# Output projection of an RG-LRU layer: the middle four of six channel groups from scaled two-byte halves

## The chip, the cores and the metric

One core of one Trainium2 chip runs the whole program. The metric is the device time of one execution in microseconds (us), taken as a median over runs. TensorE is PE in the profile (its weight loads are PEld), VectorE is DVE, ScalarE is ACT, GpSimd is POOL, and SyncE, which issues most DMA transfers, is SP.

## The reference, cut to what matters

The program computes two residual layers on a sequence of 1024 vectors of 1024 channels, and a final RMS norm. The change touches the first layer alone:

```python
def lru_mixer(h, w_in, conv_w, conv_b, wa, ba, wx, bx, a_param, w_out):   # h = rms_norm(x, g)
    u = h @ w_in                                     # 1024 -> 2 * 1536
    xb, gate = u[..., :LRU_WIDTH], u[..., LRU_WIDTH:]
    xc = causal_depthwise_conv(xb, conv_w, conv_b)   # 4 taps
    r = sigmoid(block_diag_linear(xc, wa, ba))       # 12 blocks of 128
    i = sigmoid(block_diag_linear(xc, wx, bx))
    a = exp(-LRU_C * r * softplus(-a_param))
    bterm = sqrt(1 - a * a) * (i * xc)
    hs = scan(a, bterm)                              # h_t = a_t * h_(t-1) + b_t
    y = hs * silu(gate)
    return y @ w_out                                 # 1536 -> 1024
```

All of it is float32. The second layer is attention with a forget gate, and the change leaves it alone.

## The kernel before, in words

**Precision.** Each large product of the first layer is made of three TensorE products. A float32 operand is split into a high part rounded to the four-byte type fp32r and a low part, the rest; `gemm_steps` (L141) then sums high by high, low weight by high activation, and high weight by low activation. Weights are split by a cast on ACT (`to_hi`, tile `wh`) and a subtraction (`to_lo`, tile `wl`), which POOL does for the input projection and DVE for the output projection. The second layer uses two-byte halves (fp16) scaled by bounds instead.

**Tiling.** The layer's 1536 inner channels are 12 blocks of 128, and the loop over n at L482 goes through them. Channels lie on the partitions and the 1024 positions along the free axis, in two halves of 512. A round n does this:

- `ups` of block n (the convolution's input, L490 and L504): 8 tiles of k, 2 halves and 3 products, so 48 matmuls of 128x128 by 512. `conv(n)` (L318) scales it by the row's inverse norm into `us`, and applies the four taps into `xc`.
- `gates(n-1)` (L337): 12 matmuls, and a tanh of each result on ACT (`th`, `ti`).
- `outputs(n-2)` (L383): y = a * sg on DVE, its high half `yh` by ACT and its low half `yl` by DVE.
- `gps` of block n-1 (the gate branch), 48 matmuls, `silu`, and `recur(n-1)` (L360): tanh, exp, square and sqrt on ACT, several DVE products, and the scan over the sequence on DVE (L380).

The output projection goes by groups of two blocks (`project_out(g)`, L405). A group is 16 `ops` tiles (8 output blocks, 2 halves) of 6 matmuls, each added to the residual `x` by DVE (L413). They fill the gaps between the other products: the code takes a few at a time (`take(fill, 2)`) in a later round.

`squares_of_weights` (L424) reads the second layer's weights during the first layer and sums their squares with ACT (tile `wsf`), which the second layer's scales need. It takes turns with `conv` for two small buffers (tag `wgf`). A call of `some()` (L476) brings one such step.

**What sets the order.** The framework's scheduler puts the instructions of each engine in an order from the data dependencies, from the buffers of each pool and from hints that one instruction be issued after another (`tc.issue_after`). Each engine then runs its own queue in that order. `ups` and `gps` share two PSUM tiles of two banks each (tag `S`), so `ups` of block n+1 cannot begin before DVE has read `ups` of block n. The `ops` tiles have two banks (tag `g`) and the gates two (tag `O`). The temporaries `us` and `m` (tag `m2`, the `t` of `recur`) each have one buffer.

Of the kernel before, what the change touches and what calls it, by code (L numbers as in the profile page):

```python
# [19 lines left out]
P = 128  # L20
# [7 lines left out]
GROUP = 2  # L28
ORDER = "1.v1..1.v1..00", "1.v1..1.v1..0000"
# [14 lines left out]
def trunk(ctx: ExitStack, tc: tile.TileContext, xt, w0, wg, wo0, pc, gn, gf, w1, wv, wf, bf, wo1, out):  # L44
# [163 lines left out]
    with nullcontext(ExitStack()) as l0:  # L208
# [106 lines left out]
        def product(pt, h, w):  # L315
            gemm(pt, zip(w, raw[h]))

        def conv(n, ups):  # L318
            us, xc = long("us"), long("xc", bufs=2)
# [40 lines left out]
        def recur(n, parts=(slice(0, SEQ),)):  # L360
# [4 lines left out]
            for cs in parts:  # L365
# [11 lines left out]
                with tc.issue_after(s["last"].ins):  # L377
                    nc.scalar.activation(t_, t_, AF.Sqrt, scale=1.0 / 16.0)
                nc.vector.tensor_tensor(ti, ti, t_, ALU.mult)
                nc.vector.tensor_tensor_scan(a_, a_, ti, old, ALU.mult, ALU.add)  # L380
                old = a[:, cs.stop - 1 : cs.stop]

# [22 lines left out]
        def project_out(g):  # L405

            for d0 in range(0, KT, 2):
                for db, w in enumerate(out_weights(g, d0), d0):
                    for h, cs in enumerate(halves):
                        pt = ps.tile([P, HALF], F32, tag="g", name="ops")  # L410
                        gemm(pt, zip(w, [tuple(z[:, cs] for z in p) for p in ys[2 * g : 2 * g + 2]]))
                        x = xs[h][db]
                        nc.vector.tensor_tensor(x, x, pt, ALU.add)  # L413
                        yield
# [7 lines left out]
        wsq = const.tile([P, 96], F32, name="wsq")  # L422

        def squares_of_weights():  # L424
# [8 lines left out]
            todo.append((wf, [root[:, 1:2]]))  # L433
            held = []
            for src, to in todo + [(None, None)]:
                if len(held) == 2 or src is None and held:
                    measure(*held.pop(0))
                if src is None:
                    break
                n = src.shape[1] * src.shape[2]  # L440
                wt = tmp.tile([P, HALF], F32, tag="wgf", name="wsf", bufs=2)[:, :n]
                nc.sync.dma_start(wt.rearrange("p (a b) -> p a b", b=src.shape[2]), src)
                held.append((wt, n // len(to), to))
                yield
# [37 lines left out]
        for n in range(NB):  # L482
# [7 lines left out]
            product(ups[0], 0, wu)  # L490
# [7 lines left out]
            else:  # L498
                gates(n - 1)
                if n > 1:  # L500
# [3 lines left out]
            product(ups[1], 1, wu)  # L504
# [8 lines left out]
            if n % 2 and n > 1:  # L513
# [13 lines left out]
            if n:  # L527
                drain(silu(state[n - 1], held.pop(n - 1)))

                with tc.issue_after(state[n]["tap"].ins):  # L530
                    recur(n - 1)
# [965 lines left out]
```

## Time and profile before

| what | value |
|---|---|
| median of 3 runs (lowest, highest) | 1024.79 us (1023.81, 1027.17) |
| the profiled execution's own time | 1025.09 us |
| its span, first to last instruction | 1023.2 us |
| mean granted TensorE clock | 0.995 |
| busy in the span: PE, PEld, DVE | 98%, 64%, 78% |
| busy in the span: ACT, POOL | 66%, 11% |

The first layer takes about the first 457 us. In the page, a group of instructions is named by its line, engine, operation and tiles (out<-in). In the timeline the columns are the start in us, the duration in us, the engine, the line, the operation and the tiles; a bracket at a row's end gives the engine's idle time ahead of it and what ended that. Matmuls overlap: the distance between the starts of two neighbours, called the pitch here, is what one costs TensorE, and it is shorter than the duration shown.

### The profile page before, as it was taken

The page shows a single profiled execution, that of the slowest core. Times are in us where ns is not written, and L with a number is a line of the kernel's source. Part 1 is how long each engine was busy: PE and PEld are TensorE (multiplying, and loading weights), DVE is VectorE, ACT ScalarE, POOL GpSimd, SP SyncE. Part 2 cuts the span into 40 slices and gives each one's busy share as a digit, 9 for nine tenths or more (in the row PEclk, how much of TensorE's full clock was granted, in tenths as well). Part 3 has the DMA queues.
Part 4 walks back from the last instruction along what each step waited for, and adds up shares of the span by engine and source line. Part 5 has one row for each costly group of instructions (what it writes and reads, how often), then busy time and mean ns, then how long its engine had stood idle before and what let it go on. Part 6 is the DMA issues. An engine that isn't in the chain of part 4 may idle for free.

```text
span 1023.2 us, 15101 instructions
## 1 busy us (share of the span) xinstructions
PE 999.1 (98%) x5098; PEld 656.1 (64%) x5098; DVE 794.3 (78%) x1504; ACT 672.7 (66%) x1215; POOL 110.4 (11%) x104
## 2 busy tenths in 40 slices
PE   9999999999999999999989999999999999998997
PEld 7787788788888887866545555555555555443454
DVE  7689585677558557998787889987888878995765
ACT  8469756657566667565775667766676666863555
POOL 1310221222122121000200000000010000001200
PEclk9999999999999999999999999999999999998999
DMA  7111433333334233252366677877687777778944
GB/s 254 62 52 49 140 121 107 98 119 125 98 104 149 93 106 103 80 170 95 82 156 130 119 161 153 177 155 147 134 202 138 151 140 150 155 166 183 244 78 166
DMA packets 219630, 135.88 MB, mean 133 GB/s; under 512 B 162080, under 2 KB 186464, under 8 KB 219552
## 3 DMA queue, kind: packets, MB, share of 16 engines
q1 hardware_dynamic: 216912, 126.27, 50.8%
q0 software_dynamic: 2640, 8.65, 3.3%
q8 instruction: 40, 0.66, 0.3%
q14 instruction: 38, 0.31, 0.1%
HBM read 75.16 MB, written 9.37 MB: 83 GB/s over the span
## 4 chain that ended last, share of the span: by engine, by line
PE 70%; DVE 10%; issue 8%; DMA 5%; ACT 4%; POOL 1%; SPq 1%; DVEq 0%; ACTq 0%; POOLq 0%
PE gps L72 26%; PE ops L72 14%; PE ups L72 10%; PE vps L72 7%; PE S L72 5%; PE O L72 4%; PE gate L72 2%; PE turn L72 1%; POOL wl L114 1%; DMA pT<-pp 1%; DMA wf<-in_w 1%; DVE w L733 1%; DMA wsf<-in_wo 1%; DVE h L660 1%; DVE pp L1088 1%
## 5 line engine op out<-in xcount | busy, mean ns | idle before, releaser
L72 PE MATMUL gps<-h,w 128*128 128x512 f16 x1152 | 268.1, 379 | 1.4 <-DVE qkl L902 0.7
L72 PEld LDWEIGHTS <-w 128*128 128x128 f16 x1440 | 140.6, 98 | 157.3 <-issue 7.3
L60 ACT ACTIVATE p<-p,m 128x128 f32<-128x128 f32 (+7 forms) x128 | 98.8, 772 | 74.4 <-DVE m L1075 70.1
L1075 DVE CUSTOM_DVE_ANT_0 p<-S,mask,vsq 128x128 f32<-128x128 f32 (+7 forms) x128 | 103.8, 811 | 21.1 <-PE S L72 19.6
L114 POOL TENSOR_TENSOR wl<-wf,wh 128x512 fp32r<-128x512 f32 x46 | 82.4, 1800 | 314.9 <-ACT wh L60 226.1
L60 ACT ACTIVATE pp<-p,sums 128x128 f16<-128x128 f32 (+7 forms) x128 | 97.9, 768 | 22.4 <-ACT p L60 14.5
L1088 DVE SCALAR_TENSOR_TENSOR pp<-p,sums,pp 128x128 f16<-128x128 f32 (+7 forms) x128 | 103.6, 812 | 10.9 <-ACT pp L60 10.5
L60 ACT ACTIVATE wsf<-wsf 128x512 f32<-128x512 f32 (+1 forms) x81 | 50.5, 625 | 61.7 <-DMA wsf<-in_w 33.5
L72 PEld LDWEIGHTS <-h 128*128 128x128 f16 x768 | 74.9, 98 | 21.5 <-issue 1.4
L72 PE MATMUL S<-T,U 128*128 128x512 f16 (+4 forms) x384 | 83.6, 327 | 1.4 <-DVE m L1075 1.1
L72 PE MATMUL ops<-yh,wh 128*128 128x512 f32 x192 | 76.7, 399 | 2.0 <-ACT yh L60 1.1
L72 PE MATMUL ups<-hh,wl 128*128 128x512 f32 x192 | 75.9, 395 | 0.8 <-POOL wl L114 0.8
L72 PE MATMUL ups<-hh,wh 128*128 128x512 f32 x192 | 76.4, 399 | 0.1
L72 PE MATMUL ups<-hl,wh 128*128 128x512 f32 x192 | 76.3, 397 | 0.2 <-DVE hl L275 0.2
L72 PE MATMUL ops<-yh,wl 128*128 128x512 f32 x192 | 75.7, 394 | 0.6 <-DVE wl L114 0.6
L72 PE MATMUL gps<-hh,wh 128*128 128x512 f32 x192 | 75.8, 395 | 0.0
L72 PE MATMUL gps<-hh,wl 128*128 128x512 f32 x192 | 75.5, 393 | 0.1
L72 PE MATMUL gps<-hl,wh 128*128 128x512 f32 x192 | 75.4, 393 | 0.0
L72 PE MATMUL ops<-yl,wh 128*128 128x512 f32 x192 | 74.5, 394 | 0.0
L413 DVE TENSOR_TENSOR x<-x,ops 128x512 f32<-128x512 f32 x80 | 53.7, 680 | 23.7 <-PE ops L72 23.5
L72 PE MATMUL vps<-wv,h 128*128 128x256 f16 x576 | 70.4, 273 | 0.0
L72 PE MATMUL ops<-y,w 128*128 128x512 f16 x288 | 69.2, 388 | 0.9 <-DVE sg L1044 0.9
(249 smaller groups left out, 1777.1 us busy)
## 6 DMA issues: line engine op xcount, KB each, us to landing
wf<-in_w SPq DMA_DIRECT2D x106, 256.0 KB
wsf<-in_w SPq DMA_DIRECT2D x48, 256.0 KB
wf<-in_wo SPq DMA_DIRECT2D x64, 128.0 KB
x<-in_xt SPq DMA_DIRECT2D x16, 256.0 KB
wsf<-in_wv SPq DMA_DIRECT2D x16, 256.0 KB
wsf<-in_wo SPq DMA_DIRECT2D x16, 256.0 KB
x1d<-x SPq DMA_DIRECT2D x16, 256.0 KB
T<-qkh SPq DMA_DIRECT2D x64, 64.0 KB
```

The costliest lines, as they stand in the source:

```text
L60: act[0] = op(*args, **kw)
L72: pe[0] = nc.tensor.matmul(*args, **kw)
L114: return eng.tensor_tensor(lo, src, f32(hi), ALU.subtract)
L413: nc.vector.tensor_tensor(x, x, pt, ALU.add)
L660: nc.vector.scalar_tensor_tensor(lo, x, g_, hi, ALU.mult, ALU.subtract)
L733: nc.vector.scalar_tensor_tensor(lo, wt, scale, hi, ALU.mult, ALU.subtract)
L1075: nc.vector.tensor_tensor_reduce(p, S[:, :n], mask[:, SEQ - n :], unit_s[:, pair : pair + 1], -NEG, ALU.add, ALU.min, accum_out=m)
L1088: nc.vector.scalar_tensor_tensor(both[:, :, 1], p, r, both[:, :, 0], ALU.mult, ALU.subtract)
```

## The change

Groups 1 to 4 of the output projection (blocks 2 to 9, the tuple `SCALED`) use fp16 halves; groups 0 and 5 stay as they are.

- After a = a * sg, ACT takes the absolute value of the whole row with a running sum per channel (`gate_output`). That sum gives a unit `u` per channel and its inverse. `scaled_output` makes the fp16 high half on ACT with that inverse as scale, and the low half on DVE.
- The squares of the group's weights are summed by the machinery of `squares_of_weights`: 16 more loads and 16 more squares on ACT. `weight_sum` and `weight_root` make a bound from them per partition.
- `group_scales` multiplies unit and bound, sums over all partitions by a small matmul against a tile of ones (`total`, which takes one of the two `g` banks), and derives the weights' scale and the result's unit on DVE.
- `scaled_out_weights` loads the weights as before and makes the fp16 halves with a scale per partition: two ACT casts of 256 columns and two DVE instructions in place of one of each with 512. It is called one step ahead. The eviction multiplies by the unit of the group while it adds.
- `conv`'s temporary `us` goes to the single buffer `m2` that `recur` uses. `product` calls `some` once more in its middle, for n from 3 to 10. `project_out` is made earlier in its round.

The small new tensors lie in old ones that are free by then: the channel units in `sp_d`, their inverses in `sp_q`, the weight bounds in `sp_e`, and the shares and units of a group in two columns of `pct`.

```diff
         def conv(n, ups):
-            us, xc = long("us"), long("xc", bufs=2)
+            us, xc = long("m2"), long("xc", bufs=2)
...
                 with tc.issue_after(s["last"].ins):
                     nc.scalar.activation(t_, t_, AF.Sqrt, scale=1.0 / 16.0)
+                    if root is not None:
+                        weight_root(root)
...
+        def gate_output(n):
+            s = state[n]
+            a_, u = s["a"], unit_y[:, n : n + 1]
+            nc.vector.tensor_tensor(a_, a_, s["sg"], ALU.mult)
+            last = act[0]
+            nc.scalar.activation(s["sg"], a_, AF.Abs, accum_out=u)
+            act[0] = last
+            nc.vector.tensor_scalar(u, u, 1.0 / TOP, 1e-20, ALU.mult, ALU.add)
+            nc.vector.reciprocal(inv_y[:, n : n + 1], u)
+
+        def scaled_output(n):
...
+            to_hi(y[:, 0], s["a"], nc.scalar, scale=scale)
+            nc.vector.scalar_tensor_tensor(y[:, 1], s["a"], scale, y[:, 0], ALU.mult, ALU.subtract)
...
+        def group_scales(g):
...
+            nc.vector.tensor_scalar(share[:, both], unit_y[:, both], w, None, ALU.mult)
+            total = ps.tile([P, HALF], F32, tag="g", name="total")[:, :2]
+            matmul(total, onesf, share[:, both], start=True, stop=True)
+            nc.vector.tensor_reduce(top, total, mybir.AxisListType.X, ALU.add)
+            nc.vector.reciprocal(inv, top)
+            nc.vector.tensor_scalar(share[:, both], unit_y[:, both], inv, None, ALU.mult)
...
+        def scaled_out_weights(g, d0):
...
+            for i in range(2):
+                scale = share[:, 2 * g + i : 2 * g + i + 1]
+                to_hi(hi[:, i::2], wt[:, i::2], nc.scalar, scale=scale)
+                nc.vector.scalar_tensor_tensor(lo[:, i::2], wt[:, i::2], scale, hi[:, i::2], ALU.mult, ALU.subtract)
...
                         x = xs[h][db]
-                        nc.vector.tensor_tensor(x, x, pt, ALU.add)
+                        if scaled:
+                            nc.vector.scalar_tensor_tensor(x, pt, unit_g[:, 2 * g : 2 * g + 1], x, ALU.mult, ALU.add)
+                        else:
+                            nc.vector.tensor_tensor(x, x, pt, ALU.add)
...
-            product(ups[0], 0, wu)
+            product(ups[0], 0, wu, some if 2 < n < NB - 1 else lambda: None)
             some()
...
+                if n - 2 in SCALED:
+                    gate_output(n - 2)
+                if n % 2 == 0 and n - 2 in SCALED:
+                    weight_sum(n // 2 - 1)
                 gates(n - 1)
-                if n > 1:
+                if n - 2 in SCALED:
+                    with tc.issue_after(state[n - 1]["last"].ins):
+                        scaled_output(n - 2)
+                    if n % 2:
+                        new = project_out((n - 3) // 2)
+                        next(new)
+                        fill = itertools.chain(fill, new)
+                elif n > 1:
```

The order moves with it. DVE before, around the reading of `ups` of block 2 (`us<-ups,rs` of 1024 columns; the `sp_` rows are small set-up work):

```order
58 L238 TENSOR_TENSOR sp_d<-sp_e 128x12
59 L325 SCALAR_TENSOR_TENSOR xc<-us,pct,xc 128x1022
60 L239 TENSOR_SCALAR sp_q<-sp_d 128x12
61 L325 SCALAR_TENSOR_TENSOR xc<-us,pct,xc 128x1021
62 L241 SCALAR_TENSOR_TENSOR sp_q<-sp_q,sp_d 128x12
63 L321 TENSOR_TENSOR us<-ups,rs 128x1024
```

DVE after, around the same reading, whose target is now called m_621; m_524 is the `t` of `recur(0)`, and the row `a<-a,ti` is its scan:

```order
68 L377 SCALAR_TENSOR_TENSOR m_524<-th,m_524 128x1024
69 L110 CAST wgh<-wgf 128x256
70 L115 TENSOR_TENSOR wgl<-wgf,wgh 128x256
71 L115 TENSOR_TENSOR xcl<-xc,xch 128x1024
72 L378 SCALAR_TENSOR_TENSOR ti<-ti,xc 128x1024
73 L115 TENSOR_TENSOR wl<-wf,wh 128x512
74 L384 TENSOR_TENSOR ti<-ti,m_524 128x1024
75 L358 TENSOR_TENSOR gps<-gps,rs 128x1024
76 L385 SCALAR_TENSOR_TENSOR a<-a,ti 128x1024
77 L324 TENSOR_TENSOR m_621<-ups,rs 128x1024
```

The reading of `ups` has moved behind the last use of m_524 and behind the scan.

PE before, at the end of `gps` of block 0, where `ups` of block 3 and `gates(1)` follow:

```order
262 L72 MATMUL ups<-hh,wh 128x512
263 L72 MATMUL ups<-hh,wl 128x512
264 L72 MATMUL gate<-xch,wgh 128x512
265 L72 MATMUL gate<-xch,wgl 128x512
266 L72 MATMUL ups<-hl,wh 128x512
267 L72 MATMUL gate<-xch,wgh 128x512
268 L72 MATMUL gate<-xch,wgl 128x512
269 L72 MATMUL ups<-hh,wh 128x512
```

PE after, at the same place:

```order
255 L73 MATMUL gps<-hl,wh 128x512
256 L73 MATMUL gate<-xch,wgh 128x512
257 L73 MATMUL gate<-xch,wgl 128x512
258 L73 MATMUL gate<-xch,wgh 128x512
259 L73 MATMUL gate<-xch,wgl 128x512
260 L73 MATMUL gate<-xcl,wgh 128x512 x2
261 L73 MATMUL gate<-xch,wgh 128x512
262 L73 MATMUL gate<-xch,wgl 128x512
263 L73 MATMUL gate<-xcl,wgh 128x512
264 L73 MATMUL gate<-xch,wgh 128x512
265 L73 MATMUL gate<-xch,wgl 128x512
266 L73 MATMUL gate<-xcl,wgh 128x512
```

The twelve matmuls of the gates stood between those of `ups`; now all of them come first, and `ups` of block 3 begins behind them.

ACT before, in an odd round of the loop's middle (`yh<-a` is the cast of y, `sg<-gps` the tanh of the gate branch):

```order
169 L60 ACT_TABLE_LOAD
170 L60 ACTIVATE sg<-gps 128x1024
171 L60 CAST wh<-wf 128x512
172 L60 ACTIVATE th<-gate,hba 128x512 x2
173 L60 ACTIVATE m_2092<-th,c_105 128x1024
174 L60 ACTIVATE a<-th,nc_106 128x1024
175 L60 CAST wh<-wf 128x512
176 L60 ACTIVATE th<-a 128x1024
177 L60 ACTIVATE ti<-gate,hbx 128x512 x2
178 L60 CAST yh<-a 128x1024
```

ACT after, in an odd round (`sg,sp_d<-a` is the absolute value with its sum; `w_2000` and `w_2078` are fp16 high halves of output weights, the third row from the end the cast for an input weight):

```order
190 L61 ACT_TABLE_LOAD
191 L61 ACTIVATE sg<-gps 128x1024
192 L61 ACTIVATE wsf,wsq<-wsf 128x512
193 L61 ACTIVATE sg,sp_d<-a 128x1024
194 L61 ACTIVATE th<-gate,hba 128x512 x2
195 L61 ACTIVATE a<-th,nc_106 128x1024
196 L61 ACTIVATE w_2000<-wf,pct 128x2x128 x2
197 L61 ACTIVATE wsf,wsq<-wsf 128x512 x2
198 L61 ACTIVATE w_2078<-wf,pct 128x2x128 x2
199 L61 CAST wh<-wf 128x512
200 L61 ACTIVATE ti<-gate,hbx 128x512 x2
201 L61 ACTIVATE y_1988<-a,sp_q 128x1024
```

The cast of the input weight `wh` now stands behind two steps that need the group's scales. Over the whole program ACT has 955 rows in this listing where it had 913, DVE 1511 where it had 1471, SP 598 where it had 578, and POOL as many as before; ACT's table loads are 43 rows where they were 35. The order of the second layer is almost unchanged.

More of the change, by code (lines that the diff above doesn't have):

```diff
@@ L503, in trunk @@
             some()
-            product(ups[1], 1, wu)
+            product(ups[1], 1, wu, some if 2 < n < NB - 1 else lambda: None)
             some()
@@ L512, in trunk @@
                     softplus()
-            if n % 2 and n > 1:
+            if n % 2 and n > 1 and n - 3 not in SCALED:
                 fill = itertools.chain(fill, project_out((n - 3) // 2))
```

58 lines of the change are left out of this document (51 added, 7 removed).

## The prediction

> **What bounds the kernel now.** I read the page's busy shares first, then the windows of the first layer's middle, where the changed work lies, and then the waits of PE and of ACT there.
>
> ```profile
> PE 999.1 (98%) x5098; PEld 656.1 (64%) x5098; DVE 794.3 (78%) x1504; ACT 672.7 (66%) x1215; POOL 110.4 (11%) x104
> 150.00:400.00 250.00, 249.97 (x1082) 202.78 (x1081) 163.46 (x174) 157.83 (x263) 53.13 (x28) 1.00 0.35 112
> ```
>
> The columns of the window are PE, PEld, DVE, ACT and POOL busy, the granted clock, and the DMA share. PE works 249.97 of 250 us at a granted clock of 1.00, while DVE has 163.46 (65%) and ACT 157.83 (63%). So in the middle of the layer only what shortens PE's own work can gain, and everything the other engines take over is free until PE waits for it. Between 40 and 460 us PE's waits are few:
>
> ```profile
> PE ops L72 <- ACT yh L60: 1.1, 1, 1.1
> PE ups L72 <- POOL wl L114: 0.8, 1, 0.8
> PE ops L72 <- DVE x L681: 0.7, 1, 0.7
> PE ops L72 <- DVE wl L114: 0.6, 1, 0.6
> ```
>
> Each column triple is the sum, the count and the longest wait in us. There is little to win from waits (3.2 us in these rows) and much to lose. The gain must come from TensorE's pitch.
>
> **The gain: pitch of the products.** The number of matmuls stays: a group has 8 output blocks, 2 halves and 6 matmuls, so four groups have 384. Only their type changes. These are the first `ops` of a run of twelve in fp32r and the first matmul behind the run, then a run of twelve in fp16 from the second layer, with the next row:
>
> ```profile
> 351.34 0.40 PE L72 MATMUL ops<-yh,wh 128*128 128x512 f32 x1
> ...
> 354.11 0.40 PE L72 MATMUL gps<-hh,wl 128*128 128x512 f32 x1
> 937.50 2.75 PE L72 MATMUL ops<-y,w 128*128 128x512 f16 x12
> 940.09 0.81 PE L72 MATMUL S<-T,U 128*128 128x512 f16 x4
> ```
>
> Twelve fp32r matmuls take 354.11 - 351.34 = 2.77 us, or 230.8 ns each; twelve in fp16 take 940.09 - 937.50 = 2.59 us, or 215.8 ns. The difference is 15.0 ns, and 384 x 15.0 ns = 5.8 us. Both types stream 512 columns and both rows run at nearly full clock, so this is all there is: the two-byte type does not halve anything. The bounds are 5.8 us and nothing, the second if a fp16 matmul among fp32r neighbours keeps their pitch; I take 5.8, since the run of twelve is as long as the runs that the new `ops` come in.
>
> **Loss at the beginning: `us` in m2.** With one buffer for both, DVE cannot read `ups` of block 2 before the last use of recur(0)'s m, and the order puts it behind the scan too. These are the rows of before, DVE first, then PE's first `ups` of block 3, one `wl` of POOL and one `ti` of ACT:
>
> ```profile
> 59.95 1.22 DVE L321 TENSOR_TENSOR us<-ups,rs 128x1024 f32<-128x1024 f32 x1
> 67.21 1.23 DVE L374 SCALAR_TENSOR_TENSOR m<-th,m 128x1024 f32<-128x1024 f32 x1 [1.14 <-ACT th L60]
> 70.62 0.68 DVE L114 TENSOR_TENSOR wl<-wf,wh 128x512 fp32r<-128x512 f32 x1
> 71.23 1.22 DVE L355 TENSOR_TENSOR gps<-gps,rs 128x1024 f32<-128x1024 f32 x1
> 72.36 2.18 DVE L379 TENSOR_TENSOR ti<-ti,m 128x1024 f32<-128x1024 f32 x1
> 75.66 2.28 DVE L380 TENSOR_TENSOR_SCAN a<-a,ti 128x1024 f32<-128x1024 f32 x1
> 69.94 0.40 PE L72 MATMUL ups<-hh,wh 128*128 128x512 f32 x1
> 72.17 1.29 POOL L114 TENSOR_TENSOR wl<-wf,wh 128x512 fp32r<-128x512 f32 x1 [13.55 <-ACT wh L60]
> 65.56 0.67 ACT L60 ACTIVATE ti<-gate,hbx 128x512 f32<-128x512 f32 x1
> ```
>
> Before, `us` was done at 61.17, so the PSUM tile was long free when PE came to it at 69.94. After, DVE goes through m, two products and `wl` as before until about 71.3, then the product with m (1.22, or 2.18 as here beside POOL), `gps` 1.22, the scan 2.28 and `us` 1.22, less some 0.08 of overlap each: it ends between 76.9 and 77.9. PE has the twelve matmuls of the gates in between, 12 x 0.23 = 2.8 us at the pitch above, and would be ready at 69.94 + 2.8 = 72.7. So PE stands for 4.2 to 5.2 us in all around 71 to 78; part of it may show at the gates, whose third PSUM tile waits for a tanh.
>
> Against that stands what the time buys. The chains of ACT, DVE and POOL that are late in the next two rounds have as much longer to catch up:
>
> ```profile
> 100.38 0.50 PE L72 MATMUL ops<-yh,wh 128*128 128x512 f32 x1 [1.11 <-ACT yh L60]
> 101.93 0.50 PE L72 MATMUL gate<-xch,wgh 128*128 128x512 f32 x1 [0.36 <-ACT xch L60]
> 104.63 0.50 PE L72 MATMUL ups<-hh,wl 128*128 128x512 f32 x1 [0.80 <-POOL wl L114]
> ```
>
> These waits are 1.11 + 0.36 + 0.80 = 2.27 us, and they go when PE comes four us later. Net: between 4.2 - 2.3 = 1.9 and 5.2 if none goes; the low end is 1.3, since ACT's new order makes `th`, for which DVE's m waits, ahead of this `ti` instead of behind it, 0.6 us earlier. I take 2.0, because all three waits are shorter than the delay.
>
> **The sum over the partitions (`total`).** Four small matmuls, each between long ones. The nearest row is a matmul of 8 columns:
>
> ```profile
> L72 PE MATMUL xnorm<-xsq,onesf 128*128 128x8 f32 x4 | 0.6, 214 | 0.0
> ```
>
> That is 4 x 0.2 = 0.8 us at most by its mean of 214 ns, and I take 0.7; the weight load lies behind the matmul ahead. It takes one of the two `g` banks until DVE has reduced it. What queues behind it on PE are `ops` of an earlier group, and gates and `ups` of the same round; a late reduction costs a wait that I count with the next term.
>
> **Odd rounds: what PE waits for.** Each of the rounds 5, 7, 9 and 11 starts a scaled group. Now ACT's cast of the next input weight stands behind the absolute value of y, and behind the fp16 casts, which need `total` and DVE's three small steps on it. Behind that cast wait POOL's `wl` and PE's `ups` or `gps`. A round of before shows how much room there is: POOL makes two `wl` in a row, PE's first two rows that use the first and the second are these.
>
> ```profile
> 249.61 5.34 POOL L114 TENSOR_TENSOR wl<-wf,wh 128x512 fp32r<-128x512 f32 x2 [15.90 <-ACT wh L60]
> 265.92 1.29 POOL L114 TENSOR_TENSOR wl<-wf,wh 128x512 fp32r<-128x512 f32 x1 [10.97 <-ACT wh L60]
> 253.17 0.39 PE L72 MATMUL ups<-hh,wl 128*128 128x512 f32 x1
> 255.91 0.39 PE L72 MATMUL ups<-hh,wl 128*128 128x512 f32 x1
> ```
>
> The second is there at 254.95 and wanted at 255.91: 0.96 us of room. A `wl` costs 1.29 us alone and 2.67 in this pair. If both of a round's `wl` go from the short to the long form, that is 2 x 1.38 = 2.8 us later, less the room 1.9; so a round loses between nothing and 1.9, rounded to 2.0 in what follows. I take 0.4 in each of four rounds, 1.6 in all, nearer to nothing, because PE's order leaves `ops` to run ahead of `ups`, as it did in this very pair.
>
> The trace has the lock behind the two lengths: the product `ti<-ti,m` at 72.36 took 2.18 us where a product of the same size took 1.22 at 59.95, and it ended one length behind POOL's `wl` (72.36 + 2.18 = 74.54; 72.17 + 1.29 + 1.22 = 74.68). The Trainium skill, "SBUF — State Buffer", section "SBUF: two separate sides", has it as a lock that a DVE instruction with two SBUF inputs or a GpSimd one holds for its whole length. By that rule a `wl` starts late by one scan at most, 2.28 us, so that one lost race costs 3.6 us rather than 2.67, and a round could lose 2.9 rather than 1.9.
>
> **What should cost nothing.** ACT's new work, from these rows:
>
> ```profile
> L60 ACT ACTIVATE hh<-x,gnt 128x512 fp32r<-128x512 f32 x16 | 11.1, 714 | 0.9 <-DMA x<-in_xt 0.9
> L60 ACT ACTIVATE w<-wf,outs 128x256 f16<-128x256 f32 x8 | 4.0, 495 | 0.2 <-DMA wf<-in_wo 0.2
> L60 ACT ACTIVATE wsf<-wsf 128x512 f32<-128x512 f32 (+1 forms) x79 | 49.3, 625 | 59.6 <-DMA wsf<-in_w 33.5 <-DMA wsf<-in_wo 14.8 <-DMA wsf<-in_wv 10.1
> L60 ACT CAST wh<-wf 128x512 fp32r<-128x512 f32 x56 | 33.9, 609 | 24.9 <-PE ops L72 20.8 <-issue 4.1
> L60 ACT ACTIVATION_READ_ACCUMULATOR wsf<-wsf 128x1 f32 x79 | 14.8, 187 | 0.0
> L60 ACT CAST xch<-xc 128x1024 fp32r<-128x1024 f32 x9 | 9.4, 1040 | 0.2
> L60 ACT ACT_TABLE_LOAD x21 | 26.9, 1283 | 1.9 <-DVE wsq L626 1.5
> ```
>
> Eight absolute values with their sums at 1.04 + 0.19 are 9.8 us; 16 more squares at 0.63 + 0.19 are 13.1; 16 steps of weights, each two casts of 0.495 for one of 0.609, are 6.1; eight more table loads at 1.28 are 10.3. Together 39 us over some 300 us, so that ACT goes from 63% to 76%. It is covered by the 33.5 + 14.8 + 10.1 = 58.4 us that ACT now waits for the `wsf` loads between 100 and 440 us. If that cover goes, ACT becomes late in the odd rounds first, and the loss is in the term above. A scale that lies in memory costs about 0.10 (714 against 609), which the 0.495 holds already.
>
> The next instruction begins 0.01 us after a table load (1.28 us from 246.05, the next at 247.35):
>
> ```profile
> 246.05 1.28 ACT L60 ACT_TABLE_LOAD   x1
> 247.35 1.06 ACT L60 ACTIVATE m<-m 128x1024 f32<-128x1024 f32 x1
> ```
>
> The Trainium skill, "ScalarE: Activation LUTs", section "What ACT_TABLE_LOAD costs", adds a drain of 1380 ns to the load's 1283. By it the eight loads would cost 21 us and ACT would keep 8 us of its 58 where the rows leave 19; the rows show no such gap, and the measurement decides.
>
> DVE's new work: 64 evictions of the fused form and 16 pairs of low halves.
>
> ```profile
> L413 DVE TENSOR_TENSOR x<-x,ops 128x512 f32<-128x512 f32 x80 | 53.7, 680 | 23.7 <-PE ops L72 23.5
> L1227 DVE SCALAR_TENSOR_TENSOR xh<-xh,outs,ops 128x512 f32<-128x512 f32 x13 | 9.6, 740 | 0.6 <-PE ops L72 0.6
> L733 DVE SCALAR_TENSOR_TENSOR w<-wf,outs,w 128x256 f16<-128x256 f32 x8 | 3.8, 475 | 0.0
> L1086 DVE RECIPROCAL sums<-sums 128x1 f32<-128x1 f32 x128 | 20.3, 160 | 2.4
> ```
>
> 64 x 0.06 is 3.8 us; 16 x (2 x 0.475 - 0.68) is 4.3; some 40 steps of one column at 0.16 are 6.4. That is 15 us over 300, and takes DVE from 65% to 70%. The 16 more loads of 256 KB go to a DMA system whose share is 0.35. The extra call of `some` in `product` only spreads squares that were made anyway. The last group keeps its type, so the end of the layer keeps its two waits (0.6 and 0.7 us).
>
> **The sum.** Against the profiled execution's 1025.09 us: -5.8 (pitch) + 2.0 (beginning) + 0.7 (`total`) + 1.6 (odd rounds) = -1.5, so 1023.6. The median of before is 0.30 lower than that execution, and so the forecast is 1023.3 us. About 0.3% is what a measurement of this kernel can tell from no change, 3.1 us: faster means below 1021.7, slower above 1027.9. The forecast lies within.
>
> **Rivals**, each with its time on the median's basis.
>
> - All covers hold (faster). The rounds lose nothing, `total` hides for the most part (0.2), and the beginning costs its low end, 1.3: -5.8 + 1.3 + 0.2 = -4.3, so 1020.5. For it speaks that ACT stands 58 us for loads; against it that the long form of `wl` leaves 0.96 us of room.
> - ACT and POOL set the odd rounds (slower). The cast of the input weight comes late behind `total` and the fp16 casts, POOL's `wl` then falls beside DVE's product and scan and takes its long form, and PE waits for it with `ups` behind in its queue. At the bound of 2.0 in each of four rounds: -5.8 + 2.0 + 0.7 + 8.0 = +4.9, so 1029.7. It decides from the point at which a round loses more than (3.1 + 5.8 - 2.0 - 0.7) / 4 = 1.55 us. For it speak the pairs of `wl` that take 5.34 us for two; against it that PE did not wait in any of these before.
> - The change does not do what it says: fp16 between fp32r neighbours keeps the pitch of 230.8. Then the gain is nothing and the costs stay, +4.3, so 1029.1. Only long fp16 runs are in the trace, and that is what speaks for it.
>
> **Chances.** The forecast's own case 0.41; covers hold 0.36; ACT and POOL late 0.17; no gain in pitch 0.06. That gives faster 0.36, the same 0.41, slower 0.23. The low end, 1019.0, is the first rival with nothing lost at the beginning or in `total`, so that the 5.8 us are left whole; the high end, 1028.9, takes in the forecast with its beginning at 5.2 (+3.2, 1026.5) and rounds that lose 1.0 each (+2.4), and leaves out the worst of the two slower rivals.
>
> **What would show it.** In the profile of the changed kernel: runs of `ops` in f16 with a pitch near 216 ns; a wait of PE of 4 to 5 us in sum between 70 and 79 us, put down to DVE m or ACT th, and no waits of the size of 1.11 and 0.80 in the next two rounds; four `total` of about 0.2 us; PE waits for POOL `wl` or DVE of under 0.6 us in each odd round; ACT busy near 76% in the middle. The prediction is wrong if the pitch of `ops` in f16 stays near 230, if PE's waits behind 110 us sum to more than 6 us (then the second rival holds) or to less than 0.5 with a short beginning (then the first), or if anything past the first layer changes by more than 1 us.

## The result, and the profile after

The changed kernel takes 1032.07 us (median of 6 runs, 1027.20 to 1034.89) beside 1025.21 us of the kernel before (6 runs). The ratio is 1.0061, with a 95% interval from 1.0044 to 1.0077: slower by 0.4 to 0.8%, outside the predicted range (1019.0 to 1028.9 us). The profiled execution took 1031.79 us where before's took 1025.09, and its span is 1030.0 us where it was 1023.2.

The page's busy shares and the window of 150 to 400 us, with the columns as in the prediction:

```profile
PE 997.7 (97%) x5106; PEld 619.5 (60%) x5106; DVE 806.7 (78%) x1556; ACT 706.0 (69%) x1291; POOL 91.1 (9%) x104
150.00:400.00 250.00, 244.95 (x1077) 170.74 (x1075) 174.96 (x222) 182.14 (x320) 35.69 (x27) 1.00 0.41 126
```

PE is no longer busy throughout: it misses 5 us in that window alone. DVE has gone from 163.46 to 174.96 us (70%), as costed, and ACT from 157.83 to 182.14 (73%, where 76% was costed). POOL has not become slower but faster, 35.69 us for 27 steps where it had 53.13 for 28. So the contention that the second rival feared has not come. PE's waits between 40 and 470 us say what has:

```profile
PE ops L73 <- DVE x L477: 4.4, 4, 1.5
PE ups L73 <- DVE m L324: 3.2, 1, 3.2
PE gate L73 <- ACT th L61: 1.9, 1, 1.9
PE ops L73 <- DVE wl L115: 0.6, 1, 0.6
PE gps L73 <- POOL wl L115: 0.5, 1, 0.5
...
PE total L73 <- DVE pct L411: 0.3, 1, 0.3
```

Two waits of 1.9 and 3.2 us stand at the beginning; 4.4 us go to `ops` that wait for the residual's eviction. The second layer's first `gps` begins 6.7 us later (459.43 against 452.70 us), so the whole loss lies in the first layer.

**The beginning.** The timeline of the changed kernel, DVE and then PE:

```profile
71.41 2.30 DVE L384 TENSOR_TENSOR ti<-ti,m 128x1024 f32<-128x1024 f32 x1
73.63 1.22 DVE L358 TENSOR_TENSOR gps<-gps,rs 128x1024 f32<-128x1024 f32 x1
74.76 2.28 DVE L385 TENSOR_TENSOR_SCAN a<-a,ti 128x1024 f32<-128x1024 f32 x1
76.96 1.19 DVE L324 TENSOR_TENSOR m<-ups,rs 128x1024 f32<-128x1024 f32 x1
...
73.50 0.50 PE L73 MATMUL gate<-xch,wgh 128*128 128x512 f32 x1 [1.89 <-ACT th L61]
...
78.30 0.47 PE L73 MATMUL ups<-hh,wh 128*128 128x512 f32 x1 [3.16 <-DVE m L324]
...
79.91 0.63 PE L73 MATMUL ups<-hh,wh 128*128 128x512 f32 x1
80.34 0.63 PE L73 MATMUL ups<-hh,wl 128*128 128x512 f32 x1
...
83.17 0.39 PE L73 MATMUL ups<-hl,wh 128*128 128x512 f32 x1
```

DVE's chain is the one that was worked out: `us` is done at 78.15, and PE takes up `ups` at 78.30. What was not foreseen stands behind it. From 79.9 us on the matmuls start 0.43 us apart instead of 0.23 and take 0.63 instead of 0.40, and at 83.17 it is over. From 78.30 to 83.17 PE makes 14 matmuls in 4.87 us, where 14 x 0.231 is 3.23: the wait costs 1.6 us more than its length. The window from 78 to 84 us shows it as a granted clock of 0.72.

**The odd rounds.** One of three places of the same kind, 73 us apart: ACT, DVE and PE in the changed kernel.

```profile
219.96 0.61 ACT L61 ACTIVATE wsf<-wsf 128x512 f32<-128x512 f32 x1
...
221.33 0.63 ACT L61 ACTIVATE wsf<-wsf 128x512 f32<-128x512 f32 x1 [0.67 <-DMA wsf<-in_w]
...
222.07 1.28 ACT L61 ACT_TABLE_LOAD   x1
223.37 1.06 ACT L61 ACTIVATE m<-m 128x1024 f32<-128x1024 f32 x1
...
224.46 1.23 DVE L384 TENSOR_TENSOR ti<-ti,m 128x1024 f32<-128x1024 f32 x1 [2.86 <-ACT m L61]
225.60 1.23 DVE L358 TENSOR_TENSOR gps<-gps,rs 128x1024 f32<-128x1024 f32 x1
226.73 2.28 DVE L385 TENSOR_TENSOR_SCAN a<-a,ti 128x1024 f32<-128x1024 f32 x1
228.93 1.39 DVE L477 SCALAR_TENSOR_TENSOR x<-ops,pct,x 128x512 f32<-128x512 f32 x2
...
229.71 1.02 PE L73 MATMUL ops<-y,w 128*128 128x512 f16 x4 [1.46 <-DVE x L477]
```

Read it from the bottom. PE has no free bank for `ops`. The evictions stand on DVE behind the scan, behind `gps` and the product with m. That product waits 2.86 us for ACT's square root, and ahead of the root ACT has two squares of weights, one of them with its load still on the way. At 303 us it is the same, with 0.79 us of waiting for the load. At 375 us the two squares (366.07 and 366.68) wait for no load, and DVE's product waits 2.08 us all the same: here no load, but the squares' own time (some 1.3 us for the two) stands ahead of the root.

**The pitch.** Two runs of `ops` in fp16 with the fp32r matmuls around them:

```profile
179.47 1.47 PE L73 MATMUL ops<-y,w 128*128 128x512 f16 x6
180.59 0.58 PE L73 MATMUL gps<-hl,wh 128*128 128x512 f32 x1
181.01 0.39 PE L73 MATMUL gps<-hh,wh 128*128 128x512 f32 x1
...
219.99 2.76 PE L73 MATMUL ops<-y,w 128*128 128x512 f16 x12
222.40 0.58 PE L73 MATMUL ups<-hh,wh 128*128 128x512 f32 x1
222.82 0.40 PE L73 MATMUL ups<-hh,wl 128*128 128x512 f32 x1
```

The first fp32r matmul behind a run takes 0.42 us to the next start, so run and follower have to be read together: 7 matmuls in 1.54 us where fp32r alone needs 7 x 0.231 = 1.62, and 13 in 2.83 where it needs 3.00. That is 13 and 14 ns for each fp16 matmul in these two runs. By them the type gains nearly what was forecast.

### The profile page after: what moved, and what is told of

Read it like the earlier page. It is cut to its first block, busy times and chain, and to the rows that moved or that the text cites. A ratio compares the mean times of both kernels' runs of the same rounds, so it can differ in the third digit from the quotient of the medians.

```text
span 1030.0 us, 15313 instructions
## 1 busy us (share of the span) xinstructions
PE 997.7 (97%) x5106; PEld 619.5 (60%) x5106; DVE 806.7 (78%) x1556; ACT 706.0 (69%) x1291; POOL 91.1 (9%) x104
## 4 chain that ended last, share of the span: by engine, by line
PE 54%; issue 13%; DVE 12%; ACT 9%; DMA 9%; POOL 2%; SPq 1%; ACTq 0%; POOLq 0%; DVEq 0%
PE gps L73 22%; PE ops L73 9%; PE vps L73 6%; PE S L73 5%; PE O L73 4%; PE ups L73 4%; DMA wf<-in_w 3%; DMA wsf<-in_w 2%; ACT L61 2%; ACT wsf L61 2%; POOL wl L115 2%; PE turn L73 1%; PE gate L73 1%; DMA pT<-pp 1%; DVE w L824 1%
## 5 line engine op out<-in xcount | busy, mean ns | idle before, releaser
L73 PEld LDWEIGHTS <-w 128*128 128x128 f16 x1824 | 174.4, 98 | 209.3 <-issue 25.5
L73 PE MATMUL ops<-y,w 128*128 128x512 f16 x672 | 161.4, 384 | 5.3 <-DVE x L477 4.4
L115 POOL TENSOR_TENSOR wl<-wf,wh 128x512 fp32r<-128x512 f32 x46 | 63.7, 1389 | 340.2 <-ACT wh L61 277.1
L73 PE MATMUL gps<-hh,wh 128*128 128x512 f32 x192 | 78.4, 408 | 0.0
L61 ACT ACTIVATE wsf<-wsf 128x512 f32<-128x512 f32 (+1 forms) x97 | 60.2, 622 | 26.0 <-DMA wsf<-in_w 10.8
L73 PE MATMUL O<-pT,v 128*128 128x512 f16 (+7 forms) x396 | 61.2, 326 | 6.3 <-DMA pT<-pp 6.3
L73 PEld LDWEIGHTS <-U 128*128 128x128 f16 x384 | 35.0, 98 | 39.0 <-issue 8.9
L477 DVE SCALAR_TENSOR_TENSOR x<-ops,pct,x 128x512 f32<-128x512 f32 x64 | 46.9, 742 | 6.2 <-PE ops L73 5.9
```

Of the source, the lines that this page charges most:

```text
L61: act[0] = op(*args, **kw)
L73: pe[0] = nc.tensor.matmul(*args, **kw)
L115: return eng.tensor_tensor(lo, src, f32(hi), ALU.subtract)
L477: nc.vector.scalar_tensor_tensor(x, pt, unit_g[:, 2 * g : 2 * g + 1], x, ALU.mult, ALU.add)
```

## The experiments

Each compares with runs of the kernel before on the same chip; ratios are to that kernel, with their 95% intervals. The changed kernel's ratio is 1.0061. The median of the kernel before itself lay between 1025.2 and 1022.5 us in these batches, so two experiments of different batches are compared by their ratios, of which 0.001 is 1.0 us; such a difference is known to some 2 or 3 us. The theories are: A, the buffer that `us` shares holds PE up at the beginning and is the main loss; D, squares that wait for their loads hold up ACT, and behind it DVE's scan and PE's `ops`; G, the extra call of `some` makes that happen. Their rivals are B (the added work on ACT), C (DVE's own order), F (the bank that `total` takes) and E (any new order of the queues costs, wherever it comes from).

**e2: the shared buffer alone**, in the kernel before:

```diff
-            us, xc = long("us"), long("xc", bufs=2)
+            us, xc = long("m2"), long("xc", bufs=2)
```

> The kernel before with this one edit of the change: us in the buffer of recur's m. Theory A: the waits near 71 to 79 us and the slow matmuls behind them appear as in the changed kernel, and the kernel is 4 to 7 us slower than before, 1029 to 1032 us. Rival B: the sharing alone costs less than 2 us, below 1027.5 us.

1031.68 us, ratio 1.0076 [1.0056, 1.0096]. PE's waits in it:

```profile
PE ups L72 <- DVE m L321: 2.6, 1, 2.6
PE gate L72 <- ACT th L60: 1.9, 1, 1.9
```

The waits come with this edit alone, the granted clock is 0.71 from 78 to 84 us, and the three waits of before near 100 us are gone. This one line costs as much as the whole change, within the intervals. Theory A holds here.

**e1: the changed kernel with `us` in its own buffer**, the same line the other way round.

> The changed kernel with the convolution's us in a buffer of its own again, as before the change. Theory A (the shared buffer holds TensorE up at the beginning): the two waits of 1.9 and 3.2 us between 71 and 79 us go, and with them the stretch of matmuls at 427 ns behind them (about 1.9 us), while waits like the 2.3 us of the kernel before may come back at 100 to 105 us; the time falls by 4.7 to 7.0 us against the changed kernel, to 1025 to 1027.5 us. Rival B (the squares and the scales on ScalarE are what costs): the time falls by less than 2.5 us, since a wait at the beginning only lets the others catch up.

1039.91 us, ratio 1.0155 [1.0129, 1.0180]: slower than the changed kernel, where theory A and rival B both expected a gain. The waits at the beginning are gone; in their place stand waits of 1.5 us at 147, 3.9 at 160 and 2.4 at 243 us. So the effects do not add up, and theory A alone falls.

**e3: the same scales with fp32r halves.** The core of the edit:

```diff
-            y = ypool.tile([P, 2, SEQ], FP16, tag=("yh", "yl")[n % 2], name="y16")
+            y = tuple(ypool.tile([P, SEQ], F32R, tag=z, name=z) for z in ("yh", "yl"))
...
-            both = wpool.tile([P, 2, 4, P], FP16, tag=("wh", "wl")[d0 // 2 % 2], name="w16")
-            hi, lo = both[:, 0], both[:, 1]
+            hi, lo = (wpool.tile([P, 4, P], F32R, tag=z, name=z) for z in ("wh", "wl"))
```

> The changed kernel with all its scales, sums and steps, but with the halves of y and of the output weights in the four-byte type fp32r again. It measures the type's share. If the pitch gives what the rows of before say (15 ns for each of 384 matmuls), it is 5.8 us slower than the changed kernel, 1037 to 1038.5 us. If the neighbours of another type take the gain away, it is within 1.5 us of the changed kernel, 1030.5 to 1033.5 us.

1037.03 us, ratio 1.0117 [1.0088, 1.0146]: 5.7 us above the changed kernel by ratios, with some 3 us of uncertainty either way. Its waits for x are 5.1 us in two places instead of 4.4 in four. Behind them stand 13 matmuls at half speed, where the changed kernel has such matmuls only at the beginning and e3 has none there. So the larger part of the difference is the type's; the run can't tell the 13 to 14 ns of the rows from the 15 forecast.

**e5: without the 16 added squares.**

```diff
-            for i in sorted(at_):
-                todo.insert(i, (at_[i], [wsum[:, at_[i][0], at_[i][1] // 2 : at_[i][1] // 2 + 1]]))
...
-            nc.vector.tensor_reduce(bound[:, g : g + 1], wsum[:, g], mybir.AxisListType.X, ALU.add)
+            nc.vector.tensor_reduce(bound[:, g : g + 1], onesf[:, :4], mybir.AxisListType.X, ALU.add)
```

> The changed kernel without the 16 added loads and squares of the output weights; the group's bound is made from a constant, so that the scales are other numbers and every other step stays. Theory A: the three waits of 1.4 us of ops for DVE's x behind the scan in the odd rounds come from squares that stand ahead of the square root on ScalarE, and become smaller by half or more, 2 to 4 us in all, so 1028 to 1030 us; the beginning stays as it is. Rival C (DVE's own order sets these waits): the waits stay and the time is within 1.5 us of the changed kernel.

1033.85 us, ratio 1.0100 [1.0078, 1.0122]. No gain: by ratios it is 3.9 us slower than the changed kernel. Waits of 1.3 and 1.5 us remain at 230 and 302 us, and new ones of 1.5 and 2.1 us stand at 310 (before a `total`) and 461. The added squares by themselves are not what holds the odd rounds up.

**e8: squares called later**: the two calls of `some` in the loop over the gate branch's halves are moved behind `recur`.

```diff
                 for h in range(2):
                     product(gps[:, h], h, wn)
-                    some()
...
+            if n > 1:
+                some()
+                some()
```

> The changed kernel with the two calls for squares that stood in the loop over the gate branch's halves moved behind recur, so that fewer squares can stand ahead of its square root on ScalarE; nothing else. Theory D (squares that wait for their loads hold up ScalarE's table load and square root, DVE's scan comes late behind them, and the residual's eviction behind the scan holds up TensorE): the three waits of 1.4 us become half or less, 2 to 4 us in all, 1028 to 1030 us. Rival E (any new order of the queues costs as much in another place): within 2 us of the changed kernel or slower, with new waits of over 1 us in other rounds.

1033.12 us, ratio 1.0094 [1.0077, 1.0111]. Two of the waits became 2.6 us instead of 1.4, and the third went. This is what rival E expected: moving the calls only moved the waits.

**e10, e11 and e12: no squares at all**, in the changed kernel, in the kernel before, and in e1. The edit is the same, with constants for the sums:

```diff
+            for _, to in todo:
+                for o in to:
+                    nc.vector.memset(o, 1.0)
+            return
+            yield
             held = []
```

> The changed kernel without any squares of weights in the first layer: neither the 81 of before nor the 16 added, and none of their loads; the sums are constants, so that the scales and the output are other numbers. Theory D: the waits of ops and total for DVE behind 150 us go (4.7 us), the beginning (5.1 us of waits and the slow matmuls) stays, 1026 to 1028 us. Rival E: waits of that size remain in the odd rounds, 1030 us or more.

> The control of the run without squares: the kernel before without any squares of weights and their loads, the sums being constants. TensorE waits for none of them before, so theory D expects 1023.5 to 1026 us, no change within 1.5 us. Rival E, by which any new order of the queues costs, expects 1026 us or more.

> The changed kernel with us in its own buffer and without any squares of weights and their loads; the sums are constants, so that the scales and the output are other numbers. With the squares, giving us its own buffer made the changed kernel slower (1039.9 us). Theory D (squares that wait for their loads hold up ScalarE, and a TensorE that comes earlier runs into them): without squares the buffer of its own gains what the beginning costs, 4 to 6 us against the run without squares, so 1021 to 1023 us. Rival E (a new order costs wherever it comes from): 1026 us or more, with waits in the odd rounds as before.

The changed kernel comes to 1026.84 us, ratio 1.0029 [1.0015, 1.0043]; the kernel before to 1022.13, ratio 0.9984 [0.9972, 0.9997]; e1 to 1019.61, ratio 0.9967 [0.9952, 0.9982]. All of PE's waits between 40 and 470 us that the changed kernel has left without squares are these:

```profile
PE ups L73 <- DVE m L324: 3.3, 1, 3.3
PE ops L73 <- DVE x L777: 2.5, 2, 2.1
PE gate L73 <- ACT th L61: 2.0, 1, 2.0
```

The waits in the odd rounds are gone with all the change's own work on ACT and DVE still there (absolute values, scales, `total`, fused evictions). So it is the squares, with their loads, that make them; rival B, the rest of the added work, and rival F, the bank that `total` takes, can't by themselves, for both are still there. By ratios the squares cost 1.6 us in the kernel before, 3.3 in the changed one and 19.3 in e1. In the changed kernel that is less than the waits that go, since a wait of 2.1 us stands new at 455.6 us. The 1.6 us of e11 are at the edge of what theory D allowed there (1.5). And without squares the buffer of its own gains 6.4 us (e12 beside e10), where with them it lost 9.6. Theory D foretold the sign; the time lies 1.4 us below its range.

**g1: the extra call alone**, in the kernel before:

```diff
-            gemm(pt, zip(w, raw[h]))
+            for i, _ in enumerate(gemm_steps(pt, zip(w, raw[h]))):
+                if i == 1:
+                    middle()
...
-            product(ups[0], 0, wu)
+            product(ups[0], 0, wu, some if 2 < n < NB - 1 else lambda: None)
```

and the same for the second half.

> The kernel before with one edit of the change alone: the extra call of some in the middle of product, for blocks 3 to 10; the squares are the same, they come earlier. Theory G (the extra call puts squares that wait for their loads ahead of the tanh and the square root on ScalarE): 1027 us or more, with waits of TensorE for DVE or POOL in the rounds 4 to 9. As the prediction had it (the call only spreads what is made anyway): within 1.5 us of the kernel before, 1022 to 1025.5 us.

1033.86 us, ratio 1.0107 [1.0086, 1.0128]. The same squares, called earlier, cost 11 us. The timeline of ACT ahead of PE's longest wait, and that wait:

```profile
111.73 0.63 ACT L60 ACTIVATE wsf<-wsf 128x512 f32<-128x512 f32 x1 [3.07 <-DMA wsf<-in_wv]
...
115.84 0.63 ACT L60 ACTIVATE wsf<-wsf 128x512 f32<-128x512 f32 x1 [2.88 <-DMA wsf<-in_wv]
...
119.79 0.63 ACT L60 ACTIVATE wsf<-wsf 128x512 f32<-128x512 f32 x1 [2.58 <-DMA wsf<-in_wv]
...
121.78 0.63 ACT L60 ACTIVATE wsf<-wsf 128x512 f32<-128x512 f32 x1 [1.27 <-DMA wsf<-in_wv]
...
122.41 0.67 ACT L60 ACTIVATE th<-gate,hba 128x512 f32<-128x512 f32 x1
...
123.13 0.50 PE L72 MATMUL gate<-xch,wgh 128*128 128x512 f32 x1 [2.37 <-ACT th L60]
```

ACT stands 9.8 us in its queue for four loads. The tanh of the first gate stands behind all of them, and PE waits with the third gate for the bank that this tanh frees at 123.08 us.

**e14, e13 and e15: without the added squares**, in e1 with the call (e14) and without it (e13), and in the changed kernel without the call (e15). The edits are those of e5 and the removal of `middle`.

> The changed kernel with us in its own buffer and without the 16 added squares and loads (the bound is a constant, so the scales are other numbers); the extra call stays. If the added squares are what made 1039.9 us of this kernel: 1021 to 1026 us. If the extra call is: 1032 us or more.

> The same without the extra call of some as well. Theory G: 1019 to 1024 us, near the run without any squares (1019.6 us). If the squares cost wherever they are called: 1028 us or more.

> The changed kernel (us shared) without the added squares and without the extra call. Against 1033.9 us with the call, theory G expects 1026 to 1029 us, near the run without any squares (1026.8 us); if the call is free, it stays within 1.5 us of 1033.9.

1037.32 us, ratio 1.0139 [1.0116, 1.0162]; 1032.01, ratio 1.0092 [1.0074, 1.0111]; 1036.18, ratio 1.0131 [1.0107, 1.0155]. The call costs 5 us in e14 against e13, on one chip, but taking it from the changed kernel gains nothing (e15 beside e5). The longest waits of `ops` for x are 3.6, 2.2 and 2.2 us. e13 lies 8 us above the range of theory G and e15 7 us, so the theory that the call is the cause holds in the kernel before and falls for the changed one.

**h3 and h1: more buffers for the loads**, three and four, with three loads under way:

```diff
-                if len(held) == 2 or src is None and held:
+                if len(held) == 3 or src is None and held:
...
-                wt = tmp.tile([P, HALF], F32, tag="wgf", name="wsf", bufs=2)[:, :n]
+                wt = tmp.tile([P, HALF], F32, tag="wgf", name="wsf", bufs=3)[:, :n]
```

> The changed kernel with three buffers in place of two for the loads of the squares (and of the gate's weights), and three loads under way ahead of a square; the work is the same, with all 97 squares. Theory D with the loads as the cause: ScalarE's waits for these loads fall by half or more, the waits of ops for DVE's x behind 200 us shrink with them, and the time falls to 1026 to 1029 us, near the run without any squares (1026.8 us). If ScalarE's own work is the cause: within 2 us of the changed kernel's 1032.1 us.

> The same with four buffers, and three loads under way ahead of a square. Loads as the cause: 1026 to 1029 us, and not above the run with three. ScalarE's own work as the cause: within 2 us of 1032.1 us.

With three 1039.30 us, ratio 1.0158 [1.0139, 1.0177]; with four 1029.49, ratio 1.0075 [1.0057, 1.0093]. ACT's waits for these loads between 100 and 440 us are 10.8 + 9.3 + 5.3 = 25.4 us in the changed kernel, 29.7 with three and 9.8 + 5.4 + 3.0 = 18.2 with four. Three did not take the wait away and so test nothing. Four did in part, and behind 200 us `ops` waits for x above 0.5 us only once, 0.7 us in the last group. By medians that run is 2.6 us below the changed kernel, by ratios 1.4 us above it, so no gain is shown, and whether it is the loads or the squares' own time stays open.

**e6: `total` in a bank of the gates.**

```diff
-            total = ps.tile([P, HALF], F32, tag="g", name="total")[:, :2]
+            total = ps.tile([P, HALF], F32, tag="O", name="total")[:, :2]
```

> The changed kernel with the sum over the partitions in one of the two banks of the gates instead of one of the two that ops uses. Rival F (the sum holds a bank that ops needs, and that is what ops waits for): the waits of ops for DVE behind 200 us (4.4 us) become half or less, 1028 to 1030 us. Theory D (the residual's eviction stands behind a late scan): the waits stay, within 1.5 us of the changed kernel, unless the order changes.

1050.67 us, ratio 1.0278 [1.0264, 1.0291]. Behind 200 us the waits for x are two of 0.7 us, but each scaled group now waits over 4 us for its scaled weights on ACT (17.9 us in four waits), and the matmuls behind each run slowly:

```profile
250.74 4.91 PE L73 MATMUL ops<-y,w 128*128 128x512 f16 x12 [4.54 <-ACT w L61]
255.29 0.58 PE L73 MATMUL gps<-hh,wh 128*128 128x512 f32 x1
```

Twelve matmuls in 4.55 us instead of 2.6. What the bank costs can't be read from this run, since `total` itself came later in it (at 245.93 us in place of 236.23).

**f1, f3 and f5: plain fp16, in the kernel before**: halves in fp16, high and low in one buffer, without scales, sums, the shared `us` or added work. f1 does it for groups 1 to 4. The range of fp16 is then not guarded by any bound.

```diff
+                both = wpool.tile([P, 2, 4, P], FP16, tag=("wh", "wl")[d0 // 2 % 2], name="w16")
+                hi, lo = both[:, 0], both[:, 1]
+                to_hi(hi, wt, nc.scalar)
+                nc.vector.tensor_tensor(lo, wt, hi, ALU.subtract)
```

and in the same way for y. f3 adds to it, and f5 does for all six groups:

```diff
-        weight_bounds()
+        with tc.issue_after(act[0].ins):
+            weight_bounds()
```

> The kernel before with fp16 halves of y and the output weights in groups 1 to 4, and nothing else of the change: no sums, no units and no scales, no shared buffer, no added squares; the casts, subtractions and evictions are as before, only the types differ. Theory A and D together (the type gains, the rest of the change costs): 5.8 us of pitch come through, 1018 to 1020.5 us. Rival E (the new order costs, whatever is changed): 1022 us or more, although no work was added.

> The kernel before with plain fp16 halves in groups 1 to 4, as in the run of that name, and the step that makes the second layer's bounds issued behind the last cast of y, so that its table load can't stand between the two tanh of the last block's gate. In the plain run TensorE was 2.7 us ahead of the kernel before at gps of block 9, and waited 2.5 us for yh near 422 us behind that table load. If that one place took the gain: 1021 to 1023.5 us. If other places take it: 1025 us or more.

> The same with all six groups in plain fp16. By 12.3 ns of pitch for each of 576 matmuls it gains 7.1 us in TensorE's work; with the waits of the run on four groups it comes to 1018 to 1021 us. If the new order makes waits of its own, it comes to 1024 us or more.

f1: 1026.71 us, ratio 1.0026 [1.0009, 1.0042]. Slower, with no work added. TensorE is 2.7 us ahead of the kernel before at `gps` of block 9 (342.20 against 344.94 us), with 1.4 us more of waits up to there: some 4 us gained by the type by then. At the end the gain is lost, as ACT's rows and PE's wait show:

```profile
418.74 0.60 ACT L61 ACTIVATE sg<-gps 128x512 f32<-128x512 f32 x1 [2.90 <-DVE gps L356]
420.24 1.28 ACT L61 ACT_TABLE_LOAD   x1 [0.90 <-DVE wsq L638]
421.53 0.32 ACT L61 ACTIVATE wsq<-wsq,tiny 128x28 f32<-128x28 f32 x1
421.76 0.60 ACT L61 CAST yh<-a 128x512 fp32r<-128x512 f32 x1
422.38 1.28 ACT L61 ACT_TABLE_LOAD   x1
423.67 0.60 ACT L61 ACTIVATE sg<-gps 128x512 f32<-128x512 f32 x1
...
422.41 0.80 PE L73 MATMUL ops<-yh,wh 128*128 128x512 f32 x1 [2.48 <-ACT yh L61]
```

The second layer's square root came between the last two tanh, with a table load on either side, and the cast `yh` that PE waits for stands behind the first load and the root. f3 puts the root behind: 1021.63 us, ratio 0.9990 [0.9971, 1.0009], 3.7 us better than f1 by ratios; in the traces the first layer's last `ops` begins 2.45 us earlier (457.27 against 459.72 us). Its interval holds 1, so against the kernel before no gain is shown. f5 comes to 1019.98 us, ratio 0.9976 [0.9963, 0.9990]: faster than both kernels, by 0.1 to 0.4% against the one before.

## Why the prediction was wrong

By its own steps, for the profiled execution (+6.7 us against a forecast of -1.5, so 8.2 us off). Two steps failed: the beginning was too small in the sum, and the squares' cover, priced at nothing, did not hold.

- **Pitch** (-5.8): right in kind. 13 ns in place of 15 for each of 384 matmuls is 5.0 us, and e3 agrees within its noise. The rival without a gain falls.
- **The beginning** (+2.0, between 1.3 and 5.2): the chain was right to 0.3 us, and so were the three waits that go (2.27). The waits are 1.89 + 3.16 = 5.05; with the 1.6 us of slow matmuls behind them and less the 2.27, it is 4.4. The term was mis-sized by 2.4 us, most of it the slow matmuls, of which the prediction has nothing. The traces agree: a `gps` that begins at 164.35 us before begins at 168.61 in the changed kernel and at 168.62 in e2. e2, which has this edit alone, ends 5.2 us above before by profiled executions (1030.31 against 1025.09) and 7.8 by ratios, so there more is lost later.
- **`total`** (+0.7): four sums of two matmuls each. From the matmul ahead of one to the second behind it the trace has 0.69 us (235.99 to 236.68) where two pitches are 0.46, so 0.23 each and 0.9 in all. Right in size; no run measured it by itself.
- **Odd rounds** (+1.6, by way of POOL's `wl`): the waits are 4.4 + 0.5 + 0.3 = 5.2 us, 3.6 more than the term. The place was right, the path wrong: POOL has only 0.5 of it. The rest is almost all DVE's eviction behind a scan that comes late from ACT's square root. (The bound of a round by the prediction's own numbers, 2.76 - 0.96, is 1.8, not 1.9; nothing hangs on it.) These terms make -5.0 + 4.4 + 0.9 + 5.2 = +5.5 us of the 6.7; 1.2 us are not accounted for.
- **"What should cost nothing"** is the step whose mechanism failed. It held that ACT's 58.4 us of waits for `wsf` loads cover new work, and that the extra call of `some` only spreads squares that are made anyway. It did say that ACT would be late in the odd rounds if the cover went, but put nothing in the sum for it. In the changed kernel 25.4 of the 58.4 us are still there, and PE waits all the same: as the rows of g1 show, ACT takes its queue in order, so both a square and its wait for a load are time in which everything behind waits too. The runs without squares show that the odd rounds' waits are the squares' and not the change's other work. For the call, g1 shows the price in the kernel before, 11 us; in the changed kernel neither the call nor the added squares are the cause alone (e5, e15).
- The three rivals: the slower one named the result's sign and 1029.7 us, and its sign came too (PE's waits behind 110 us sum to 6.6 us, above 6). But its lock between POOL and DVE did not decide, so that was luck. The faster one falls with the odd rounds' waits.

The runs without squares let the loss be split in one order of edits, by ratios. From e11 to e12 the type, the scales and their work gain 1.7 us, which is within the noise; from e12 to e10 the shared buffer costs 6.4; and the squares cost 1.7 more in the changed kernel than in the one before. In this order the beginning is the largest part of the loss. In another order the parts are others, for what the prediction treated as a sum is none: the same line costs some 8 us in the kernel before and saves some 9 in the changed one (e2, e1), and without squares it costs again (e10 beside e12). f1, which changes only the halves' type and their buffer, points at a reason: each edit gives each queue another order, and the kernel before has an order in which PE never waits more than 1.1 us up to 460 us. Why squares cost 19 us in e1 and 3 us in the changed kernel stays open: e13 to e15 say it is neither the added squares nor the extra call alone, and h3 and h1 don't settle that it is the loads.

## What to carry to other kernels

An engine's waits are not spare time when its queue runs in order: ask what stands behind the waiting instruction, and price optional work by that. Optional work is what need not be done at this place, like the squares here. Where a scheduler makes the order, a gain in one engine's work is worth only what the new order leaves, so try the gain alone first (here the plain type, f1 to f5), look at the one or two places where the order went wrong, and pin those. A wait on TensorE of about two microseconds or more can cost more than its length, as the beginning shows here.

## What the runs showed of the hardware

- Behind a wait of TensorE of 1.9 us or more, some 7 matmuls often ran at half speed (0.43 us from start to start in place of 0.23), for about 3 us: behind 2.37 and 2.21 us in g1, behind 2.20 in e13, behind all four of 4.3 to 4.5 in e6, and six behind 1.89 in e6 too, but not behind 2.59 and 2.54 in e8, 3.13 in e3 nor 1.89 in the changed kernel. Behind single waits of 1.0 to 1.8 us in the first layer it was never seen. The Trainium skill, "TensorE: Matmul & The Clock Gate", section "Wait — 56ns, not 53.3ns?", gives 426.7 ns for a 512-column matmul at the cold clock, and the rows agree (0.43). The Trainium skill, "TensorE: Matmul & The Clock Gate", section "HAM oscillation — how this bites in real kernels", has the rule that there be no idle gaps over about 3.4 us; here single waits of 1.9 to 2.4 us were enough, and the measurement decides.
- The first fp32r matmul behind fp16 ones takes 0.58 us and 0.42 to the next start, where others have 0.40 and 0.23. With the run ahead of it, which looks shorter by as much, this made 13 ns of gain per matmul in a run of six and 14 in a run of twelve, not 15.
